# Hybrid trunk on one core: the modulation beside the MLPs becomes row products on VectorE, and the MLP down products come two up products later

## The chip, the cores and the metric

The kernel runs on one core of one Trainium2 chip, as one launch. The metric is the device time of that core in microseconds (us); the median of three runs of the kernel before is 2835.36 us.

## The reference

A trunk of two layers over 256 tokens with 2048 features, in fp32. Each layer is a token mixer (layer 0: sparse attention, called DSA; layer 1: RWKV-7 time mixing), followed by an MLP with 8192 hidden features and a squared ReLU. Every sub-layer reads a norm of x that is shifted and scaled, and what it gives is gated and added to x. The shifts, scales and gates (the modulation, six parts of 2048 numbers a layer) come from one vector c of 2048 numbers:

```python
def block(x, c, mix, ada_w, ada_b, w1, w2):       # cut to what matters here
    sh1, sc1, g1, sh2, sc2, g2 = split(silu(c) @ ada_w + ada_b, 6)   # ada_w: 2048 x 12288
    x = x + g1 * mix(rms_norm(x) * (1 + sc1) + sh1)
    h = rms_norm(x) * (1 + sc2) + sh2
    return x + g2 * (square(relu(h @ w1)) @ w2)                      # w1: 2048 x 8192, w2: 8192 x 2048
```

So ada_w (100.7 MB a layer) is read once for a product with a single row, and w1 and w2 (67.1 MB each a layer) are read once for products with 256 rows.

## The kernel before, in words

**Phases.** The program runs through five phases: `dsa` (with the modulation that layer 0 needs first), `mlp0`, `project` and `scan` (the RWKV mixer), `mlp1`. The features lie across the 128 partitions, 16 tiles of x with 256 tokens each. A scheduler of the framework orders the instructions of every engine ahead of the launch, by priorities that follow the order of the code and by a timeline that it models; at run time each engine takes its instructions strictly in that order. All weight loads are issued by SyncE (SP), in its order too.

**Products.** A weight chunk comes from HBM in 128x512 pieces of 256 KB (tiles `raw` and `more`). Each piece is split into a high part, which ScalarE casts (`whi`, L87), and a low part, which VectorE or GpSimd subtracts (`wlo`, L89; in the MLPs the last two of a chunk's four pieces go to GpSimd, `g=(2, 3)`; some split buffers bear the names `xhi` and `xlo`). A moving tile has a high and a low half too, and each 128-row step of a product is three matmuls (L182 to L184: high x high, high x low, low x high). A product of an MLP sums 16 such steps, 48 matmuls, in one bank of PSUM (`ps_d`, `ps_m`, `ps_a` or `ps_b`).

**The MLP.** Four blocks of 2048 hidden features follow one another; in each, 16 up products (w1) make 16 hidden tiles, and then 16 down products (w2) read all 16 of them. An up product is followed on VectorE and ScalarE by a chain: scale by the tokens' 1/rms (L370), ReLU (L371), square in full (L372) and as a high part (L374), low part (L375). A down product ends in an add into `y` (L384). An MLP is 4 x 32 x 48 = 6144 matmuls.

**The modulation.** `ada_block` makes 512 of the 12288 numbers. Its ada_w block comes in eight loads of 512 KB (`araw`). Of a block there are two ways. The "array" way makes 16 matmuls on TensorE with c as the stationary operand (L215), then a transpose and a few small products. The "vector" way makes 16 multiply-adds over 128x512 into `acc`: the first on ScalarE (L217), 15 on VectorE (L219); then a 32x32 block transpose (L228), a sum (L233), four small products on TensorE (L237) and the add of a bias (L240, in two parts of six also L242). In `dsa` every third block goes the vector way; beside the MLPs all do: 24 blocks beside `mlp0` (the last part of layer 0, and five parts of layer 1) and 4 beside `mlp1`. A queue of generators feeds them in: before each MLP product, `ada_due` adds 0.8 (mlp0) or 0.2 (mlp1) steps, a step being a quarter of a block.

Of the kernel before, what the change touches and what calls it, by code (L numbers as in the profile page):

```python
# [7 lines left out]
F32 = mybir.dt.float32  # L8
F32R = mybir.dt.float32r
# [7 lines left out]
P = 128  # L17
# [21 lines left out]
ADA_INDEX, ADA_TOPK, ADA_HEAD, ADA_OUT = 2, 6, 2, 3    # steps of the modulation beside a step of the DSA mixer  # L39
TAIL = "dcm"        # banks of the DSA mixer's last output products  # L40
# [19 lines left out]
# columns of the constants kept for the whole launch, and of those of the DSA mixer alone  # L60
# [15 lines left out]

class Weights:
    """A chunk of weights as high and low parts, in pieces of up to 512 columns."""
# [18 lines left out]
class Trunk:  # L97
    def __init__(s, ctx, tc, io):
# [17 lines left out]
        s.turn, s.kinds, s.ada_kind = 0, "d", "j"  # L116
# [38 lines left out]
    # weights: a chunk of up to 2048 columns, split exactly in two parts  # L155
    def raw(s, ap, own=True):
        if not own and s.bufs["m"]:
            t = s.tp.tile([P, 1024], F32, name="araw", bufs=s.bufs["m"])
        else:
            s.raws += 1  # L160
            if s.raws % (NRAW + s.bufs["q"]) < NRAW:
                t = s.wp.tile([P, 512], F32, name="raw", bufs=NRAW)[:, :ap.shape[-1]]
            else:
                t = s.tp.tile([P, 512], F32, name="more", bufs=s.bufs["q"])[:, :ap.shape[-1]]
        s.nc.sync.dma_start(t, ap)
        return t
# [32 lines left out]
    # modulation: c_act @ ada_w, four feature tiles at a time  # L199
    def ada_block(s, layer, part, j, where):  # L200
        # where the products are made: in the array, on VectorE, or on ScalarE and GpSimd
        nc = s.nc
        blk = part * 4 + j
        array = where == "array"
        if array:
            # partial sums in the four column tiles of the array
            p = s.bank(s.ada_kind)
        acc = None if array else s.tp.tile([P, 512], F32, name="acc", bufs=1 + (s.bufs["m"] > 2))
        for q in range(4):
            w = [s.raw(s.io["ada_w"][layer, blk, q, :, i * 1024:(i + 1) * 1024], False) for i in range(2)]  # L210
            for k in range(4):
                c = s.cact[:, q * 4 + k:q * 4 + k + 1]
                wk = w[k // 2][:, k % 2 * 512:k % 2 * 512 + 512]
                if array:
                    nc.tensor.matmul(p[k * 32:k * 32 + 32, :], c.to_broadcast([P, 32]), wk, start=q == 0, stop=q == 3)  # L215
                elif q == 0 and k == 0:
                    nc.scalar.activation(acc, wk, AF.Copy, scale=c)  # L217
                elif where == "vector":
                    nc.vector.scalar_tensor_tensor(acc, wk, c, acc, op0=OP.mult, op1=OP.add)  # L219
                else:  # L220
                    t = s.A()
                    nc.scalar.activation(t, wk, AF.Copy, scale=c)
                    nc.gpsimd.tensor_tensor(acc, acc, t, op=OP.add)
            if q < 3:
                yield
        # sums over the partitions: by blocks of 32 on VectorE, then of the four blocks
        t = s.tp.tile([P, 512], F32, name="act", bufs=1)
        nc.vector.transpose(t, p if array else acc)  # L228
        if array:
            t = t.rearrange("p (f c i)->p c f i", c=4, i=32)[:, :, :, 0]  # L230
        else:
            r = s.small(16)
            nc.vector.tensor_reduce(r, t.rearrange("p (b i)->p b i", i=32), axis=AX.X, op=OP.add)  # L233
            t = r.rearrange("p (f c)->p c f", c=4)
        p = s.bank(s.ada_kind)
        for c in range(4):
            nc.tensor.matmul(p[c * 32:c * 32 + 32, :4], s.cv("i32"), t[:, c, :], start=True, stop=True)  # L237
        o = part * 16 + j * 4
        dst = s.mod[layer][:, o:o + 4]
        nc.vector.tensor_tensor(dst, p[:, :4], s.v(f"ada_b{layer}", o, 4), op=OP.add)  # L240
        if part in (1, 4):
            nc.vector.tensor_scalar(dst, dst, 1.0, None, op0=OP.add)  # L242
        yield

    def ada_enqueue(s, layer, parts, where=("vector",)):
        for p in parts:
            for j in range(4):
                s.adaq.append(s.ada_block(layer, p, j, where[j % len(where)]))
# [9 lines left out]
    # 1 / sqrt(sum / n + eps) of sums [128 tokens, w] in PSUM  # L258
# [14 lines left out]
    def spread(s, r, w, kind="m"):  # L273
        # [128 tokens, 2 tiles x w] -> [128 features, 256 tokens], w values over 128 / w features each
# [22 lines left out]
    def rms(s, n, sq):  # L297
        # 1 / rms by token, in every partition; sq: squares
# [9 lines left out]
    def modulated(s, layer, base, i, rb):  # L308
        # x * rstd * (1 + scale) + shift, split
# [27 lines left out]
    def mlp(s, layer):  # L337
        nc = s.nc
        s.kinds = "dcm"
        # the tokens' 1 / rms goes to the products, so that they can start before it is known; the shift  # L340
        # is a further column
# [16 lines left out]
        y = [s.tp.tile([P, S], F32, name=f"y{f}") for f in range(NF)]  # L358
        for b in range(4):
            hid = []  # L360
            for f in range(16):
                w = s.wload(s.io["mlp_w1"][layer, b * 16 + f])
                s.ada_due()
                p = s.dense(w, h, cols)
                if b == f == 0:
                    nc.scalar.copy(rb, s.rms(D, [s.ssq, s.lsq]))
                u, r, q = s.B(), s.B(), s.B()
                c = s.small(1)
                nc.scalar.copy(c, p[:, S:S + 1])
                nc.vector.tensor_tensor(u, p[:, :S], rb, op=OP.mult)  # L370
                nc.scalar.activation(r, u, AF.Relu, bias=c)  # L371
                nc.vector.tensor_tensor(q, r, r, op=OP.mult)  # L372
                t = s.O() if 1 < f < 2 + NO else s.A(F32R)
                nc.scalar.activation(t[:, :S], r, AF.Square)  # L374
                nc.vector.tensor_tensor(t[:, S:], q, t[:, :S].bitcast(F32), op=OP.subtract)  # L375
                hid.append(t)
            for f in range(16):
                w = s.wload(s.io["mlp_w2"][layer, b, f])
                s.ada_due()
                p = s.dense(w, hid, cols)  # L380
                if b == 0:
                    nc.scalar.copy(y[f], p)
                else:
                    nc.vector.tensor_tensor(y[f], p, y[f], op=OP.add)  # L384
                if b == 3:
                    nc.vector.scalar_tensor_tensor(s.x[f], y[f], s.m(layer, 5, f), s.x[f], op0=OP.mult, op1=OP.add)
                    s.tally(f)
# [844 lines left out]
```

## Time and profile before

| what | before |
|---|---|
| median of 3 runs | 2835.36 us (2834.36 to 2837.69) |
| span of the profiled execution | 2835.9 us (no separate time is given for it) |
| TensorE busy | 2666.8 us, 94% |
| VectorE busy | 2009.3 us, 71% |
| ScalarE busy | 1330.1 us, 47% |
| GpSimd busy | 1252.3 us, 44% |
| moved by DMA | 621.70 MB, mean 219 GB/s |

Busy shares are means over five phases with different limits, so the views by stage count for more than this table. A busy time holds also what an instruction waits once it has begun, for a port for example. PE is TensorE, DVE VectorE, ACT ScalarE, POOL GpSimd, SP SyncE.

### The profile page before, as it was taken

To read this page: it belongs to the slowest core of one execution; us is meant where nothing else is said; L and a number is where in the kernel's file an instruction comes from. 1 tells how busy PE (TensorE), PEld (TensorE's weight loads), DVE (VectorE), ACT (ScalarE), POOL (GpSimd) and SP (SyncE) were. 2 spreads that over 40 slices of the span, in tenths; PEclk is the share of its full clock that TensorE was granted. 3 is DMA by queue.
4 is the path that set the end of the run, shared out by engine and by line. 5 is a ranking of instruction groups with operands and counts; after the bars stand their busy time and mean duration, and the time that the engine had idled before them with its cause. 6 is when DMAs were issued, how large, how long until landed. Compare 5 with 4: busy or idle time off the path is not lost. (4 is left out here: it accounts for less than half of the span.)

```text
span 2835.9 us, 65852 instructions
## 1 busy us (share of the span) xinstructions
PE 2666.8 (94%) x25132; PEld 2460.3 (87%) x25132; DVE 2009.3 (71%) x3475; ACT 1330.1 (47%) x2879; POOL 1252.3 (44%) x1121
## 2 busy tenths in 40 slices
PE   7989998899999999998989899999898999999998
PEld 4566688899999999997978788888798999999998
DVE  2276658999999999948887656766798264473653
ACT  3334345445444544446655334444445454454553
POOL 1343237445454454455665412323554444444443
PEclk9998999999999999999999879999999999999999
DMA  9987836999899899854657632333577656555563
GB/s 356 367 305 289 297 106 197 299 312 332 290 302 318 291 312 318 268 174 127 201 174 224 190 91 77 105 113 89 157 262 239 193 182 183 182 182 185 182 182 115
DMA packets 290847, 621.70 MB, mean 219 GB/s; under 512 B 32353, under 2 KB 46049, under 8 KB 290529
## 3 DMA queue, kind: packets, MB, share of 16 engines
q1 hardware_dynamic: 283616, 604.89, 66.0%
q10 hardware_dynamic: 6912, 12.59, 1.2%
q8 instruction: 197, 3.23, 0.5%
q14 instruction: 122, 0.99, 0.1%
HBM read 600.57 MB, written 16.78 MB: 218 GB/s over the span
## 5 line engine op out<-in xcount | busy, mean ns | idle before, releaser
L89 POOL TENSOR_TENSOR wlo<-raw,whi 128x512 fp32r<-128x512 f32 x364 | 515.9, 1423 | 616.5 <-ACT whi L87 439.3
L87 ACT CAST whi<-raw 128x512 fp32r<-128x512 f32 x856 | 516.4, 617 | 453.5 <-PE ps_d L183 158.7
L89 DVE TENSOR_TENSOR wlo<-raw,whi 128x512 fp32r<-128x512 f32 x492 | 412.5, 842 | 236.2 <-ACT whi L87 226.4
L219 DVE SCALAR_TENSOR_TENSOR acc<-araw,cact,acc 128x512 f32<-128x512 f32 x465 | 476.2, 1025 | 8.1 <-ACT acc L217 4.4
L89 POOL TENSOR_TENSOR wlo<-more,whi 128x512 fp32r<-128x512 f32 x181 | 256.0, 1416 | 312.8 <-ACT whi L87 201.2
L87 ACT CAST whi<-more 128x512 fp32r<-128x512 f32 x366 | 223.2, 617 | 218.6 <-PE ps_d L183 75.5
L182 PE MATMUL ps_d<-A,whi 128*128 128x256 f32 x1058 | 312.7, 297 | 12.4 <-ACT B L849 4.6
L183 PE MATMUL ps_d<-A,whi 128*128 128x256 f32 x1058 | 306.1, 290 | 5.7 <-DVE A L196 5.1
L184 PE MATMUL ps_d<-A,wlo 128*128 128x256 f32 x1058 | 303.8, 287 | 0.0
L89 DVE TENSOR_TENSOR wlo<-more,whi 128x512 fp32r<-128x512 f32 (+1 forms) x185 | 152.1, 824 | 141.9 <-ACT whi L87 139.3
L182 PEld LDWEIGHTS ps_d<-A,whi 128*128 128x128 f32 x1058 | 206.0, 195 | 33.3 <-issue 6.5
L183 PEld LDWEIGHTS ps_d<-A,whi 128*128 128x128 f32 x1058 | 206.9, 196 | 10.4 <-DVE A L196 9.0
L184 PEld LDWEIGHTS ps_d<-A,wlo 128*128 128x128 f32 x1058 | 206.5, 195 | 1.4 <-issue 1.4
L183 PE MATMUL ps_d<-h,whi 128*128 128x258 f32 x552 | 157.9, 286 | 2.9 <-DVE h L352 2.8
L184 PE MATMUL ps_d<-h,wlo 128*128 128x258 f32 x552 | 156.8, 284 | 1.9 <-DVE wlo L89 1.9
L182 PE MATMUL ps_d<-h,whi 128*128 128x258 f32 x552 | 157.7, 286 | 0.0
L371 ACT ACTIVATE B<-B,sm 128x256 f32<-128x256 f32 x128 | 65.0, 508 | 197.1 <-DVE B L370 197.0
L182 PE MATMUL ps_m<-h,whi 128*128 128x258 f32 x536 | 153.2, 286 | 0.0
L183 PE MATMUL ps_m<-h,whi 128*128 128x258 f32 x536 | 152.6, 285 | 0.0
L184 PE MATMUL ps_m<-h,wlo 128*128 128x258 f32 x536 | 151.6, 283 | 0.0
L182 PE MATMUL ps_m<-A,whi 128*128 128x256 f32 x510 | 145.6, 286 | 5.4 <-DVE B L372 4.4
L183 PE MATMUL ps_m<-A,whi 128*128 128x256 f32 x510 | 145.0, 284 | 1.5 <-DVE A L375 1.5
(555 smaller groups left out, 8753.1 us busy)
## 6 DMA issues: line engine op xcount, KB each, us to landing
araw<-ada_w_in SPq DMA_DIRECT2D x384, 512.0 KB, 6.3
raw<-mlp_w_in SPq DMA_DIRECT2D x614, 256.0 KB, 4.0
more<-mlp_w_in SPq DMA_DIRECT2D x410, 256.0 KB, 4.2
raw<-b_w_r_in SPq DMA_DIRECT2D x64, 256.0 KB, 3.6
raw<-b_w_k_in SPq DMA_DIRECT2D x64, 256.0 KB, 4.0
raw<-b_w_v_in SPq DMA_DIRECT2D x64, 256.0 KB, 3.7
raw<-b_w_o_in SPq DMA_DIRECT2D x64, 256.0 KB, 3.5
hd<-A ACTq DMA_DIRECT2D x48, 256.0 KB, 4.7
```

The source lines that it names most:

```text
L87: t.nc.scalar.copy(hi[:, :n], r)
L89: e.tensor_tensor(lo[:, :n], r, hi[:, :n].bitcast(F32), op=OP.subtract)
L182: mm(out, wh, m[:, :w], start=i == 0, stop=False)
L183: mm(out, wh, m[:, w:], start=False, stop=False)
L184: mm(out, wl, m[:, :w], start=False, stop=i == n - 1)
L219: nc.vector.scalar_tensor_tensor(acc, wk, c, acc, op0=OP.mult, op1=OP.add)
L371: nc.scalar.activation(r, u, AF.Relu, bias=c)
```

## The change

1. A block of ada_w that went the vector way is now laid out by rows: one of its 512 outputs to a partition, four times over, and its 2048 inputs along the free axis (the host lays the weights out so). `spread_c` broadcasts c to all partitions once in each of three phases and makes silu(c) there, 128x2048 (`cb`). Four row products (`tensor_tensor_reduce`, 128x2048 by `cb`, summed along the row) and one add of the bias then make a block, all on VectorE. The blocks that go the array way stay there, and no block changes its way between the array and VectorE.
2. All ada_w loads are 1 MB (128x2048) in place of 512 KB; the buffers `araw` are 4 of 8 KB a partition in `dsa` in place of 9 of 4 KB, and 2 of 8 KB beside the MLPs in place of 4 of 4 KB.
3. In the MLPs the first two up products of the next block come ahead of a block's 16 down products (`AHEAD_UP = 2`), in the first three of the four blocks.

```diff
+def ada_by_row(layer, part, j):
+    return layer == 1 or part == 5 or (part > 1 and j == 2)
...
+    def spread_c(s):
+        nc = s.nc
+        s.cb = s.tp.tile([P, D], F32, name="cb", bufs=1)
+        nc.sync.dma_start(s.cb, s.io["c"].partition_broadcast(P))
+        sg = s.tp.tile([P, D], F32, name="araw", bufs=s.bufs["m"])
+        nc.scalar.activation(sg, s.cb, AF.Sigmoid)
+        nc.vector.tensor_tensor(s.cb, s.cb, sg, op=OP.mult)
...
+        for k in range(4):
+            w = s.tp.tile([P, D], F32, name="araw", bufs=s.bufs["m"])
+            nc.sync.dma_start(w, s.io["ada_w"][layer, o // 4, k])
+            if by_row:
+                nc.vector.tensor_tensor_reduce(out=w, in0=w, in1=s.cb, scale=1.0, scalar=0.0, op0=OP.mult, op1=OP.add,
+                                               accum_out=acc[:, k:k + 1])
...
+            for f in range(AHEAD_UP if b else 0, 16):
+                up(b, f)
+            for f in range(AHEAD_UP if b < 3 else 0):
+                up(b + 1, f)
+            for f in range(16):
+                down(b, f)
...
-        with t.phase("mlp0", a=14, b=12, w=2, m=4, q=MORE, g=(2, 3)):
+        with t.phase("mlp0", a=14, b=12, w=2, m=2, q=MORE, g=(2, 3)):
+            t.spread_c()
```

The functions `up` and `down` hold what stood in the two loops of `mlp`. Line numbers move by the edit: L89 becomes L94, L182 to L184 become L184 to L186, L370, L372 and L375 become L374, L376 and L379; L224 is the row product, L246 the add of the bias.

How the scheduler orders it, at two places. The first is the order on VectorE some 15 up products into `mlp0`. `acc` and `act` are tiles of the modulation, `sm` its sums, `mod` the finished numbers. Before:

```order
L228 STREAM_TRANSPOSE act<-acc 128x512
L372 TENSOR_TENSOR B<-B 128x256
L219 SCALAR_TENSOR_TENSOR acc<-araw,cact,acc 128x512
L375 TENSOR_TENSOR A<-B,A 128x256
L89 TENSOR_TENSOR wlo<-raw,whi 128x512
L219 SCALAR_TENSOR_TENSOR acc<-araw,cact,acc 128x512
L233 TENSOR_REDUCE sm<-act 128x16
```

And of the change (`ISA` is the row product and the reading of its sum):

```order
L224 ISA araw,sm<-araw,cb 128x2048
L224 ISA sm 128x1
L376 TENSOR_TENSOR B<-B 128x256
L246 TENSOR_TENSOR mod_84<-sm,vec 128x4
L94 TENSOR_TENSOR wlo<-raw,whi 128x512
L379 TENSOR_TENSOR A<-B,A 128x256
```

The transpose and the sum are gone, and so is the hand-over to TensorE that followed them. This is what stood on TensorE before where a block's sums came in, amid the 48 matmuls of an up product:

```order
L182 MATMUL ps_d<-h,whi 128x258
L237 MATMUL ps_j<-sm,cst 32x4 x4
L183 MATMUL ps_d<-h,whi 128x258
L184 MATMUL ps_d<-h,wlo 128x258
L182 MATMUL ps_d<-h,xhi 128x258
```

There are 24 such places in `mlp0` and 4 in `mlp1`, and none in either MLP of the change. The second place is on TensorE, where the up products of block 0 of `mlp0` end (`h` are the tiles that up products read, `A` and `o` the hidden tiles that down products read). Before, the bank `ps_d_6574` takes the last up product:

```order
L182 MATMUL ps_d_6574<-h_5022,whi_6568 128x258
L183 MATMUL ps_d_6574<-h_5022,whi_6568 128x258
L184 MATMUL ps_d_6574<-h_5022,wlo_6569 128x258
L182 MATMUL ps_b_6667<-A_5242,whi_6634 128x256
L183 MATMUL ps_b_6667<-A_5242,whi_6634 128x256
```

And of the change, where `ps_d_6266` takes the last up product of block 0, and `ps_b_6354` and `ps_m_6441` the two of block 1:

```order
L186 MATMUL ps_d_6266<-h_4801,wlo_6261 128x258
L184 MATMUL ps_b_6354<-h_4786,whi_6326 128x258
...
L184 MATMUL ps_m_6441<-h_4801,whi_6432 128x258
L185 MATMUL ps_m_6441<-h_4801,whi_6432 128x258
L186 MATMUL ps_m_6441<-h_4801,wlo_6433 128x258
L184 MATMUL ps_d_6528<-A_5021,whi_6501 128x256
```

Between a block's last up product and its first down product there now stand 96 matmuls.

## Rows read from the trace of the kernel before

**Rows 1.** Windows by stage: span, busy (x count) by engine, clock, DMA share, GB/s.

```profile
0.00:141.80 141.80, 114.89 (x720) 65.66 (x721) 37.45 (x84) 48.33 (x97) 36.94 (x40) 0.99 0.98 361
...
470.50:1281.60 811.10, 769.26 (x6345) 761.98 (x6346) 753.93 (x972) 388.62 (x774) 404.30 (x279) 0.97 0.88 288
...
2047.50:2822.20 774.70, 760.43 (x6258) 757.15 (x6256) 450.50 (x609) 388.05 (x763) 362.45 (x289) 0.98 0.61 192
```

**Rows 2.** Windows, a modulated stretch in which TensorE never stands.

```profile
600.00:728.00 128.00, 128.00 (x1087) 127.40 (x1087) 123.09 (x143) 64.37 (x125) 66.27 (x43) 1.00 0.95 325
```

**Rows 3.** Waits of TensorE in mlp0: us, times, longest.

```profile
PE ps_j L237 <- DVE sm L233: 30.3, 10, 5.0
...
PE ps_b L182 <- ACT A L374: 1.8, 1, 1.8
PE ps_d L182 <- ACT A L374: 1.4, 1, 1.4
PE ps_m L183 <- DVE A L375: 1.4, 1, 1.4
```

**Rows 4.** Timeline of TensorE at one such wait: start, us.

```profile
540.51 0.28 PE L182 MATMUL ps_d<-h,whi 128*128 128x258 f32 x1
545.76 0.29 PE L237 MATMUL ps_j<-sm,cst 128*32 128x4 f32 x8 [4.96 <-DVE sm L233]
545.98 0.58 PE L183 MATMUL ps_d<-h,whi 128*128 128x258 f32 x1
```

**Rows 5.** Timeline of VectorE at the same place.

```profile
539.59 0.70 DVE L228 STREAM_TRANSPOSE act<-acc 128x512 f32<-128x512 f32 x1
540.22 1.48 DVE L372 TENSOR_TENSOR B<-B 128x256 f32<-128x256 f32 x1
...
542.28 1.48 DVE L375 TENSOR_TENSOR A<-B,A 128x256 fp32r<-128x256 f32 x1
...
544.94 0.67 DVE L233 TENSOR_REDUCE sm<-act 128x16 f32<-128x512 f32 x1
```

**Rows 6.** Windows of 12 us behind waits, three of mlp0 and one of mlp1.

```profile
545.76:557.76 12.00, 12.00 (x88) 11.98 (x89) 12.00 (x19) 6.44 (x14) 4.25 (x3) 0.79 0.92 289
579.50:591.50 12.00, 12.00 (x106) 11.98 (x107) 11.96 (x18) 6.10 (x14) 5.61 (x4) 1.00 0.89 294
...
1172.49:1184.49 12.00, 12.00 (x83) 11.98 (x84) 10.74 (x18) 6.50 (x14) 3.87 (x3) 0.73 0.86 267
...
2176.30:2188.30 12.00, 12.00 (x81) 11.51 (x82) 11.69 (x15) 5.75 (x11) 4.62 (x4) 0.75 0.88 267
```

**Rows 7.** Groups of VectorE in mlp0: busy, mean ns, idle before.

```profile
L219 DVE SCALAR_TENSOR_TENSOR acc<-araw,cact,acc 128x512 f32<-128x512 f32 x359 | 369.2, 1028 | 4.6 <-ACT acc L217 1.8
...
L228 DVE STREAM_TRANSPOSE act<-acc 128x512 f32<-128x512 f32 x24 | 16.9, 703 | 0.3
L233 DVE TENSOR_REDUCE sm<-act 128x16 f32<-128x512 f32 x24 | 16.2, 676 | 0.2
```

**Rows 8.** GpSimd's splits in mlp0: min/median/max ns.

```profile
L89 POOL TENSOR_TENSOR wlo<-raw,whi x151: 1274/1511/2108, 480.7 to 1268.4; 128x512 fp32r<-128x512 f32 x151
```

**Rows 9.** Groups of VectorE in attention: a multiply with a sum.

```profile
L633 DVE CUSTOM_DVE_ANT_0 lg<-ps_m,A 128x256 f32<-128x256 f32 x16 | 6.7, 419 | 0.0
...
L633 DVE CUSTOM_DVE_ANT_0 lg<-ps_m,A 128x128 f32<-128x128 f32 x16 | 4.5, 284 | 6.9 <-PE ps_m L628 6.8
...
L633 DVE DVE_READ_ACCUMULATOR2_ANT sm<- 128x1 f32 x32 | 2.6, 82 | 0.0
```

**Rows 10.** Waits of SP's queue within mlp0.

```profile
SPq L165 <- DVE acc L219: 119.7, 120, 3.2
```

**Rows 11.** Waits of TensorE in mlp1.

```profile
PE ps_m L182 <- DVE B L372: 4.4, 1, 4.4
```

**Rows 12.** Groups of VectorE where mlp1 starts.

```profile
L219 DVE SCALAR_TENSOR_TENSOR acc<-araw,cact,acc 128x512 f32<-128x512 f32 x14 | 14.9, 1073 | 0.0
```

**Rows 13.** ScalarE's casts in attention.

```profile
L87 ACT CAST whi<-raw 128x512 fp32r<-128x512 f32 x72 | 42.6, 619 | 37.3 <-PE ps_d L183 18.9 <-issue 8.6 <-PE ps_a L183 2.7
```

More of the change, by code (lines that the diff above doesn't have):

```diff
@@ L39 @@
 ADA_INDEX, ADA_TOPK, ADA_HEAD, ADA_OUT = 2, 6, 2, 3
+AHEAD_UP = 2
 TAIL = "dcm"
@@ L115, in __init__ @@
         s.flip = s.raws = s.pieces = 0
-        s.turn, s.kinds, s.ada_kind = 0, "d", "j"
+        s.turn, s.kinds = 0, "d"
         s.due = s.rate = 0.0
@@ L153, in m, with raw @@
         return s.mod[layer][:, part * 16 + i:part * 16 + i + 1]
-    def raw(s, ap, own=True):
-        if not own and s.bufs["m"]:
-            t = s.tp.tile([P, 1024], F32, name="araw", bufs=s.bufs["m"])
-        else:
[L160 to L164, printed above, removed]
+    def raw(s, ap):
+        s.raws += 1
+        if s.raws % (NRAW + s.bufs["q"]) < NRAW:
+            t = s.wp.tile([P, 512], F32, name="raw", bufs=NRAW)[:, :ap.shape[-1]]
+        else:
+            t = s.tp.tile([P, 512], F32, name="more", bufs=s.bufs["q"])[:, :ap.shape[-1]]
         s.nc.sync.dma_start(t, ap)
@@ L197, in split @@
         return t
-    def ada_block(s, layer, part, j, where):
+    def spread_c(s):
         nc = s.nc
[L203 to L224, printed above, removed]
@@ new lines, in spread_c, with ada_block @@
+        s.cb = s.tp.tile([P, D], F32, name="cb", bufs=1)
[3 more added lines that the diff above has]
+        nc.vector.tensor_tensor(s.cb, s.cb, sg, op=OP.mult)
+    def ada_block(s, layer, part, j):
+        nc = s.nc
+        o = part * 16 + j * 4
+        by_row = ada_by_row(layer, part, j)
+        if by_row:
+            acc = s.small(4)
+        else:
+            p = s.bank("j")
+        for k in range(4):
+            w = s.tp.tile([P, D], F32, name="araw", bufs=s.bufs["m"])
+            nc.sync.dma_start(w, s.io["ada_w"][layer, o // 4, k])
+            if by_row:
+                nc.vector.tensor_tensor_reduce(out=w, in0=w, in1=s.cb, scale=1.0, scalar=0.0, op0=OP.mult, op1=OP.add,
+                                               accum_out=acc[:, k:k + 1])
+            else:
+                for q in range(4):
+                    c = s.cact[:, k * 4 + q:k * 4 + q + 1]
+                    nc.tensor.matmul(p[q * 32:q * 32 + 32, :], c.to_broadcast([P, 32]), w[:, q * 512:(q + 1) * 512],
+                                     start=k == 0, stop=k == 3)
+            if k < 3:
@@ L225, in ada_block @@
                 yield
-        t = s.tp.tile([P, 512], F32, name="act", bufs=1)
-        nc.vector.transpose(t, p if array else acc)
-        if array:
+        if not by_row:
+            t = s.tp.tile([P, 512], F32, name="act", bufs=1)
+            nc.vector.transpose(t, p)
             t = t.rearrange("p (f c i)->p c f i", c=4, i=32)[:, :, :, 0]
-        else:
-            r = s.small(16)
-            nc.vector.tensor_reduce(r, t.rearrange("p (b i)->p b i", i=32), axis=AX.X, op=OP.add)
-            t = r.rearrange("p (f c)->p c f", c=4)
@@ L235, in ada_block @@
[L235 to L242, printed above, removed]
+            p = s.bank("j")
+            for c in range(4):
+                nc.tensor.matmul(p[c * 32:c * 32 + 32, :4], s.cv("i32"), t[:, c, :], start=True, stop=True)
@@ L243, in ada_block, with ada_enqueue @@
+            acc = p[:, :4]
+        dst, b = s.mod[layer][:, o:o + 4], s.v(f"ada_b{layer}", o, 4)
+        if part in (1, 4):
+            nc.vector.scalar_tensor_tensor(dst, acc, 1.0, b, op0=OP.add, op1=OP.add)
+        else:
+            nc.vector.tensor_tensor(dst, acc, b, op=OP.add)
         yield
-    def ada_enqueue(s, layer, parts, where=("vector",)):
+    def ada_enqueue(s, layer, parts):
         for p in parts:
             for j in range(4):
-                s.adaq.append(s.ada_block(layer, p, j, where[j % len(where)]))
+                s.adaq.append(s.ada_block(layer, p, j))
@@ L358, in mlp, with up @@
         y = [s.tp.tile([P, S], F32, name=f"y{f}") for f in range(NF)]
+        hid = {}
+        def up(b, f):
+            w = s.wload(s.io["mlp_w1"][layer, b * 16 + f])
+            s.ada_due()
+            p = s.dense(w, h, cols)
+            if b == f == 0:
+                nc.scalar.copy(rb, s.rms(D, [s.ssq, s.lsq]))
+            u, r, q = s.B(), s.B(), s.B()
+            c = s.small(1)
+            nc.scalar.copy(c, p[:, S:S + 1])
+            nc.vector.tensor_tensor(u, p[:, :S], rb, op=OP.mult)
+            nc.scalar.activation(r, u, AF.Relu, bias=c)
+            nc.vector.tensor_tensor(q, r, r, op=OP.mult)
+            t = s.O() if 1 < f < 2 + NO else s.A(F32R)
+            nc.scalar.activation(t[:, :S], r, AF.Square)
+            nc.vector.tensor_tensor(t[:, S:], q, t[:, :S].bitcast(F32), op=OP.subtract)
+            hid[b, f] = t
@@ L359, in mlp, with down @@
+        def down(b, f):
+            w = s.wload(s.io["mlp_w2"][layer, b, f])
+            s.ada_due()
+            p = s.dense(w, [hid[b, k] for k in range(16)], cols)
+            if b == 0:
+                nc.scalar.copy(y[f], p)
+            else:
+                nc.vector.tensor_tensor(y[f], p, y[f], op=OP.add)
+            if b == 3:
+                nc.vector.scalar_tensor_tensor(s.x[f], y[f], s.m(layer, 5, f), s.x[f], op0=OP.mult, op1=OP.add)
+                s.tally(f)
         for b in range(4):
-            hid = []
+            for f in range(AHEAD_UP if b else 0, 16):
+                up(b, f)
+            for f in range(AHEAD_UP if b < 3 else 0):
+                up(b + 1, f)
@@ L361, in mlp @@
             for f in range(16):
[L362 to L387, printed above, removed]
+                down(b, f)
@@ L478, in dsa @@
             for part in (1, 0):
-                s.adaq.append(s.ada_block(0, part, j, "array"))
+                s.adaq.append(s.ada_block(0, part, j))
             s.ada(4)
@@ L490, in dsa @@
             raw.append(t)
-        s.ada_enqueue(0, [2, 3, 4], ("array", "array", "vector"))
+        s.ada_enqueue(0, [2, 3, 4])
         def lowrank(raw, n, gname):
@@ L1087, in build @@
         t.start()
-        with t.phase("dsa", a=27, b=17, m=9, q=MORE, g=(1, 2)):
+        with t.phase("dsa", a=27, b=17, m=4, q=MORE, g=(1, 2)):
+            t.spread_c()
             t.dsa()
@@ L1105, in build @@
         t.rate = 0.2
-        with t.phase("mlp1", a=14, b=12, w=2, m=4, q=MORE, g=(2, 3)):
+        with t.phase("mlp1", a=14, b=12, w=2, m=2, q=MORE, g=(2, 3)):
+            t.spread_c()
             t.mlp(1)
@@ L1180, in layout @@
     a["kidx_ln"] = ct(np.stack([g["a_kidx_ln_g"][0], g["a_kidx_ln_b"][0]], 1))
-    a["ada_w"] = ct(g["ada_w"].reshape(2, 4, 4, P, 24, 512).transpose(0, 4, 1, 3, 2, 5)).reshape(2, 24, 4, P, 2048)
+    aw = g["ada_w"]
+    rows = aw.transpose(0, 2, 1).reshape(2, 24, 4, P, D)
+    cols = aw.reshape(2, 4, 4, P, 24, 512).transpose(0, 4, 1, 3, 2, 5).reshape(2, 24, 4, P, D)
+    a["ada_w"] = np.stack([np.stack([(rows if ada_by_row(l, b // 4, b % 4) else cols)[l, b] for b in range(24)])
+                           for l in range(2)])
+    a["c"] = ct(g["c"].reshape(-1))
     a["mlp_w1"] = np.stack([tiles(w, 16, P) for w in g["mlp_w1"]])
```

2 lines of the change are left out of this document (1 added, 1 removed).

## The prediction, made before the changed kernel was run

> **What bounds the kernel now.** I read the windows by stage first [rows 1]. Two stages hold changed work for hundreds of microseconds: mlp0, 811.1 us with TensorE busy for 769.3, and mlp1, 774.7 us with TensorE busy for 760.4. Both make the same 6144 matmuls, so what mlp0 takes more, 36 us, is what the modulation costs beside it. The reader should see in the same row that VectorE is busy for 753.9 of mlp0's 811.1 us, nearly as long as TensorE, and that DMA runs at a share of 0.88; in mlp1, with a sixth of the modulation, VectorE has 450.5 and DMA 0.61.
>
> Then TensorE's waits within mlp0 [rows 3]. One line stands out: the four small products L237 wait ten times for the sum L233, 30.3 us in all, up to 5.0 us. Three waits of 1.4 to 1.8 us come where a block's up products end and its down products begin (for L374 and L375); the rest is small. The timelines of one such place say why it lasts. TensorE stands from 540.8 to 545.8 amid the 48 matmuls of an up product [rows 4], as L237 is placed there and the order can't be left. VectorE transposes at 539.59 but reaches L233 only at 544.94, since five other instructions stand in between, two of them on 128x256 for 1.48 us each [rows 5]. So TensorE waits for VectorE's queue, not for the modulation's arithmetic.
>
> Last, the windows of 12 us behind these waits [rows 6]. The one at 579.5 keeps the clock (1.00) and holds 106 matmuls; the one at 545.76 has a granted clock of 0.79 and 88, the one at 1172.49 has 0.73 and 83. I looked at the ten behind the ten waits: the counts lie between those two ends, and together lack about 118 matmuls, at 0.12 us each some 14 us. A wait here costs its own length and half as much again at the lower clock.
>
> **What the change removes.** In mlp0: (a) the L237 waits, 30.3 us; nothing in the MLPs of the change hands a modulation sum to TensorE, so the whole line goes. (b) The small products themselves: 24 places of 0.22 us (545.76 to 545.98 [rows 4]), 5.3 us. (c) The low clock behind (a), 14 us. (d) The waits at three block boundaries, 1.8 + 1.4 + 1.4 = 4.6 us: they lie in the first three blocks, where 96 matmuls (11.5 us) now stand between the last up product and the first reader of its tile. In mlp1: (e) the boundary wait of 4.4 us [rows 11], in block 0, and some 3 us of its low clock (81 matmuls against 106 [rows 6]). (f) Where mlp1 starts, VectorE makes 14 multiply-adds for 14.9 us in the first 35 us [rows 12] between the tiles h that TensorE waits for; the change has one 128x2048 multiply there and puts the row products later. I take 4 us, between 0 (the multiply costs as much) and 6.7 (all waits for h in that stage). Sum removed: 30.3 + 5.3 + 14 + 4.6 + 7.4 + 4 = 65.6 us.
>
> **What it adds.** (g) A row product of 128x2048. Nearest rows: a multiply with a sum takes 419 ns over 256 columns and 284 over 128, and 82 for reading the sum [rows 9]; the slope is 1.055 ns a column, so an estimate of 0.284 + 1920 x 0.00105 = 2.31 us, and 0.08. Its inputs there are one from PSUM and one from SBUF, here both from SBUF; four multiply-adds at their mean of 1.03 us in mlp0, waits included [rows 7], give 4.1 us as an upper bound. I take 2.9 us, the estimate with 0.5 us of waiting, since 3.75 multiply-adds become one instruction and so fewer are caught by GpSimd. VectorE in mlp0 then has 753.9 - 369.2 (L219) - 16.9 (L228) - 16.2 (L233) = 351.6, plus 96 x 2.9 = 278: 630 us of a stage of some 760, in place of 754 of 811. At 4.1 us a piece it has 745, and only from (811 - 351.6) / 96 = 4.8 us would VectorE alone need as long as the stage takes now. So the row products lie beside TensorE's matmuls; if that cover went, each 0.1 us of a row product would cost 9.6 us. (h) c is loaded once more in attention's start, where DMA is full (0.98, 361 GB/s): 1 MB, 2.9 us on the path. (i) Sigmoid and multiply of 128x2048 in mlp0's start: at four casts of 0.619 us [rows 13] and an estimate of 2.3 us, they stand in VectorE's queue between the updates of x that TensorE's last attention products and the first tiles h need. I take 2.5 us, between 0 (VectorE has room there) and 5. In mlp1 the same is within (f). (j) New waits of TensorE where VectorE's queue holds two row products in a row: 9 us, between 0 and 45 (as many and as costly as (a) with (c)). I take the low end's side, for the split tiles of an MLP hold ten pieces, two and a half products of 5.8 us, and PSUM has six banks for products, so a delay of 3 to 6 us is mostly covered, unlike L237, which had no cover at all. Sum added: 2.9 + 2.5 + 9 = 14.4 us. Costs nothing: the reshaped loads of attention, the same bytes in half as many instructions, and as many products of the array way.
>
> **Sum.** 2835.9 (span of the profiled execution, 0.5 us above the median, so no correction) - 65.6 + 14.4 = 2784.7; I forecast 2784 us.
>
> **A rule that speaks against it.** In the rows, a VectorE multiply-add has a mean of 1028 ns in mlp0 [rows 7] and a GpSimd split one of 1511 at the median against 1274 at best [rows 8]; so the two engines hold each other up. The Trainium skill, page "SBUF — State Buffer", section "Who interferes with whom", says that a VectorE instruction with two SBUF inputs and a GpSimd instruction that reads SBUF exclude each other, and whichever starts first keeps the shared ports for its whole length. By that rule a row product of 2.3 us would hold a split for up to 2.3 us where a multiply-add held it for 0.7; the spread of the splits (1274 to 2108) agrees with the rule for holds of 0.7 us, and no run here shows longer ones. By the rule the sum moves toward the first rival below; by the rows alone the elements that pass (24 blocks of 8192 columns in place of 7680) hold the ports about as long in total as now.
>
> **Rivals.** *The waits only move.* GpSimd's splits come late behind row products, and TensorE waits for `wlo` where it waited for L237. For it: VectorE was busy nearly throughout, and the order has row products in pairs. Against it: GpSimd is busy for 404 of 811 us [rows 1], no split is among the long waits of TensorE [rows 3]. If half of (a) and (c) comes back, 22 us beyond (j)'s middle: about 2807 us.
>
> *The loads starve TensorE (slower).* SP issues all loads in order, and with two buffers of 1 MB an ada_w load waits in its queue until the row product before last is done, with the weights behind it; already now SP waits 120 times for L219, 119.7 us [rows 10], each a hold of 1 us, and would wait longer for one instruction of 2.9 us. TensorE without gaps needs 325 GB/s at a DMA share of 0.95 [rows 2]. The modulated stretch moves 226 MB (120 products with 1.05 MB of weights each and 96 loads of 1.05 MB), 697 us at 325 GB/s. At 300 it takes 755 us, which gives 2784 + 58 = 2842 us; it decides below 305 GB/s, and the stage's own mean is 288 now. Against it: attention's start shows 361 GB/s [rows 1], and the loads have 1 MB each.
>
> *The row product is slow (slower).* At two cycles a column, 4.6 us and waits of 0.6, VectorE has 351.6 + 96 x 5.3 = 860 us in mlp0, and the kernel takes about 2880 us. Against it: the slope over columns in [rows 9].
>
> *Nothing changes*: other waits of mlp0 grow until VectorE's length sets the stage again, at 4.8 us a row product: 2836 us.
>
> **How the numbers follow.** A change of 0.2% (5.7 us) is about what a measurement of this kernel can tell from none. Forecast, 2766 to 2800: 0.56. Better still (j near 0 and the array part quicker): 0.04. Waits only move, 2800 to 2829: 0.22. Within 0.2%: 0.06. Loads starve: 0.07. Slow row product: 0.05. So faster 0.82, same 0.06, slower 0.12. The range takes the forecast's cases from 2764 and most of the moved waits, up to 2824.
>
> **What would show it.** Right: mlp0 near 765 us, no wait of TensorE for a modulation sum, granted clock 0.99 or 1.00 within mlp0, row products of 2.3 to 3 us, VectorE near 630 us there, no waits of TensorE at the first three boundaries of either MLP, mlp1 near 763. Wrong: waits of TensorE for `wlo` or for weights' DMA of tens of microseconds in mlp0; SP waiting for the row product while ScalarE waits for `raw`; row products above 4 us; attention longer by more than 5 us.

## The result, and the profile after

The changed kernel takes 2787.81 us (median of 4 runs, 2783.42 to 2791.43) where the kernel before takes 2836.53: a ratio of 0.983, with a 95% interval of 0.980 to 0.985. Measured again (experiment e8) the same kernel gave 0.981 (0.979 to 0.984). The forecast was 2784 us. The sum was right; the experiments show that a large step behind it was not.

The windows by stage after the change (attention, mlp0, the RWKV mixer, mlp1; columns as in [rows 1]; each MLP runs from the first product that reads an `h` tile to the sums of squares behind its last product):

```profile
0.00:460.90 460.90, 402.21 (x2820) 298.19 (x2820) 234.38 (x549) 182.50 (x411) 155.43 (x167) 0.94 0.78 286
460.90:1242.30 781.40, 753.77 (x6156) 749.57 (x6157) 716.57 (x751) 371.00 (x762) 495.01 (x281) 0.98 0.87 301
1242.30:2020.70 778.40, 722.02 (x9683) 647.44 (x9681) 549.41 (x1294) 372.16 (x921) 315.21 (x391) 0.93 0.46 138
2020.70:2775.00 754.30, 750.99 (x6216) 750.23 (x6217) 449.54 (x573) 383.29 (x759) 378.90 (x283) 1.00 0.62 196
```

By the same marks the stages before were 470.5, 811.5, 765.5 and 774.2 us. So mlp0 is 30.1 us shorter (forecast: 46), mlp1 19.9 (forecast: 11), attention 9.5 (forecast: 5 longer), and the mixer 12.9 longer, whose code no edit touches (e8 and the text under the table come back to it). VectorE has 717 us in mlp0 where 630 were forecast, and GpSimd went from 404 [rows 1] to 495 us, with one split more (254).

The waits of TensorE in mlp0 after the change (us, times, longest), which answer to [rows 3]:

```profile
PE ps_b L184 <- ACT A L378: 5.3, 1, 5.3
PE ps_d L186 <- DVE wlo L94: 5.3, 3, 2.2
PE ps_m L186 <- DVE wlo L94: 3.7, 1, 3.7
PE ps_d L185 <- DVE h L356: 3.7, 5, 1.6
PE ps_a L185 <- DVE h L356: 2.9, 1, 2.9
PE ps_a L186 <- DVE wlo L94: 2.7, 1, 2.7
```

No wait for a modulation sum is left. The 5.3 us are the boundary of the last block, which has no up products ahead; some 12 us are waits for low parts of weights, of which [rows 3] has none of that size.

VectorE's splits in mlp0 before, and then VectorE's and GpSimd's groups after the change, which answer to [rows 7] and [rows 8] (in the last two fences: min/median/max ns):

```profile
L89 DVE TENSOR_TENSOR wlo<-raw,whi 128x512 fp32r<-128x512 f32 x157 | 148.8, 950 | 24.7 <-ACT whi L87 24.7
```

```profile
L224 DVE CUSTOM_DVE_ANT_0 araw<-araw,cb 128x2048 f32<-128x2048 f32 x96 | 270.7, 2830 | 4.3 <-DMA araw<-ada_w_in 4.3
L94 DVE TENSOR_TENSOR wlo<-raw,whi 128x512 fp32r<-128x512 f32 x157 | 161.3, 1034 | 20.6 <-ACT whi L92 19.0 <-DMA more<-mlp_w_in 1.6
```

```profile
L224 DVE CUSTOM_DVE_ANT_0 araw<-araw,cb x96: 2276/2876/3392, 484.4 to 1184.6; 128x2048 f32<-128x2048 f32 x96
```

```profile
L94 POOL TENSOR_TENSOR wlo<-raw,whi x152: 1287/1740/3438, 460.6 to 1228.8; 128x512 fp32r<-128x512 f32 x152
```

A row product takes 2.28 us at best and 2.83 in the mean: the forecast took 2.31 and 2.9. But the splits of GpSimd now take up to 3.44 us where 2.11 was the longest [rows 8], and VectorE's own splits went from a mean of 950 to 1034 ns. One place shows it (start, duration), TensorE, VectorE and GpSimd:

```profile
582.80 0.28 PE L185 MATMUL ps_d<-o,whi 128*128 128x256 f32 x1
585.27 0.39 PE L186 MATMUL ps_d<-o,wlo 128*128 128x256 f32 x1 [2.19 <-DVE wlo L94]
```

```profile
577.92 3.38 DVE L224 CUSTOM_DVE_ANT_0 araw<-araw,cb 128x2048 f32<-128x2048 f32 x1
...
581.24 3.37 DVE L224 CUSTOM_DVE_ANT_0 araw<-araw,cb 128x2048 f32<-128x2048 f32 x1
...
584.53 0.68 DVE L94 TENSOR_TENSOR wlo<-raw,whi 128x512 fp32r<-128x512 f32 x1
```

```profile
577.78 4.67 POOL L94 TENSOR_TENSOR wlo<-raw,whi 128x512 fp32r<-128x512 f32 x2 [0.33 <-ACT whi L92]
```

Two row products start while GpSimd splits; each takes 1.1 us more than its shortest, and GpSimd's two splits take 4.67 us where two at their best take 2.6. The low part that TensorE needs stands behind them. This is the rule of the Trainium skill (page "SBUF — State Buffer", section "Who interferes with whom") that the prediction weighed: a VectorE instruction with two SBUF inputs contends with a GpSimd instruction that reads SBUF, and the ports that they share are an exclusive lock. The trace agrees, and shows that a whole instruction can be waited for: the longest split is now 2.15 us over its shortest, about one row product (2.28), and was 0.83 over it before, about one multiply-add (0.75 in e12).

### The profile page after: what moved, and what is told of

Its sections match the earlier page's. It is cut to its first block, busy times and chain, and to the rows that moved or that the text cites. A ratio compares the mean times of both kernels' runs of the same rounds, so it can differ in the third digit from the quotient of the medians.

```text
span 2788.7 us, 64443 instructions
## 1 busy us (share of the span) xinstructions
PE 2630.8 (94%) x24884; PEld 2446.9 (88%) x24884; DVE 1957.3 (70%) x3183; ACT 1309.4 (47%) x2852; POOL 1345.3 (48%) x1121
## 5 line engine op out<-in xcount | busy, mean ns | idle before, releaser
L94 POOL TENSOR_TENSOR wlo<-raw,whi 128x512 fp32r<-128x512 f32 x364 | 587.1, 1622 | 544.5 <-ACT whi L92 417.2
L94 DVE TENSOR_TENSOR wlo<-raw,whi 128x512 fp32r<-128x512 f32 x492 | 436.5, 892 | 222.6 <-ACT whi L92 211.0
L94 POOL TENSOR_TENSOR wlo<-more,whi 128x512 fp32r<-128x512 f32 x181 | 263.7, 1460 | 322.7 <-ACT whi L92 165.6
L224 DVE CUSTOM_DVE_ANT_0 araw<-araw,cb 128x2048 f32<-128x2048 f32 x124 | 342.6, 2776 | 4.6 <-DMA araw<-ada_w_in 4.6
L184 PE MATMUL ps_d<-A,whi 128*128 128x256 f32 x1058 | 309.4, 293 | 10.6 <-ACT B L863 6.2
L186 PE MATMUL ps_d<-A,wlo 128*128 128x256 f32 x1058 | 303.1, 287 | 0.5 <-DVE wlo L94 0.5
L94 DVE TENSOR_TENSOR wlo<-more,whi 128x512 fp32r<-128x512 f32 (+1 forms) x185 | 174.3, 943 | 138.8 <-ACT whi L92 135.6
L184 PEld LDWEIGHTS ps_d<-A,whi 128*128 128x128 f32 x1058 | 205.4, 195 | 26.2 <-ACT B L863 7.2
L186 PEld LDWEIGHTS ps_d<-A,wlo 128*128 128x128 f32 x1058 | 205.5, 194 | 1.5 <-DVE wlo L94 0.7
L375 ACT ACTIVATE B<-B,sm 128x256 f32<-128x256 f32 x128 | 65.3, 510 | 247.5 <-DVE B L374 247.4
L186 PE MATMUL ps_d<-h,wlo 128*128 128x258 f32 x552 | 155.8, 282 | 2.5 <-DVE wlo L94 2.4
L184 PE MATMUL ps_d<-h,whi 128*128 128x258 f32 x552 | 156.7, 284 | 0.0
L184 PE MATMUL ps_m<-h,whi 128*128 128x258 f32 x540 | 153.4, 284 | 0.0
L186 PE MATMUL ps_m<-h,wlo 128*128 128x258 f32 x540 | 152.1, 282 | 0.0
L376 DVE TENSOR_TENSOR B<-B 128x256 f32<-128x256 f32 x128 | 111.5, 871 | 52.9 <-ACT B L375 52.9
L184 PE MATMUL ps_m<-A,whi 128*128 128x256 f32 x506 | 145.1, 287 | 1.1 <-ACT whi L92 1.1
```

Source lines behind the costliest of these rows:

```text
L94: e.tensor_tensor(lo[:, :n], r, hi[:, :n].bitcast(F32), op=OP.subtract)
L184: mm(out, wh, m[:, :w], start=i == 0, stop=False)
L186: mm(out, wl, m[:, :w], start=False, stop=i == n - 1)
L224: nc.vector.tensor_tensor_reduce(out=w, in0=w, in1=s.cb, scale=1.0, scalar=0.0, op0=OP.mult, op1=OP.add, accum_out=acc[:, k:k + 1])
```

## The experiments

All use the whole kernel and the reference's inputs; e6 alone leaves out a part of the result. Ratios are to the kernel before, measured beside them.

| kernel | attention | mlp0 | mixer | mlp1 | VectorE busy in mlp0 | ratio (95%) |
|---|---|---|---|---|---|---|
| before | 470.5 | 811.5 | 765.5 | 774.2 | 753.9 | 1 |
| the change | 460.9 | 781.4 | 778.4 | 754.3 | 716.6 | 0.983 (0.980 to 0.985) |
| e1 change, nothing ahead | 459.9 | 798.8 | 769.8 | 760.4 | 674.6 | 0.990 (0.988 to 0.992) |
| e2 before, two ahead | 463.9 | 814.2 | 767.8 | 773.3 | 758.4 | 1.002 (1.0005 to 1.004) |
| e3 before, hand-over later | 468.6 | 821.6 | 767.7 | 773.8 | 750.8 | 1.005 (1.003 to 1.007) |
| e4 before, 1 MB loads | 462.4 | 813.0 | 781.4 | 771.4 | 754.7 | 1.002 (1.001 to 1.004) |
| e5 = e2 + e3 | 471.0 | 814.4 | 770.5 | 772.6 | 757.6 | 1.001 (1.0002 to 1.003) |
| e6 change, no row products | 454.7 | 749.9 | 772.4 | 755.0 | 402.2 | 0.970 (0.968 to 0.973) |
| e7 change, last boundary split | 460.7 | 780.7 | 780.2 | 755.2 | 718.9 | 0.983 (0.980 to 0.985) |
| e8 change again | 466.8 | 783.4 | 765.5 | 755.0 | 715.5 | 0.981 (0.979 to 0.984) |
| e9 change, splits on VectorE | 466.4 | 746.9 | 762.8 | 753.0 | 644.6 | 0.971 (0.968 to 0.973) |
| e10 change, square on ScalarE | 460.9 | 775.1 | 783.3 | 756.1 | 690.8 | 0.980 (0.978 to 0.982) |
| e11 before, square on ScalarE | 472.4 | 793.3 | 771.2 | 774.8 | 720.4 | 0.995 (0.994 to 0.997) |
| e12 before, splits on VectorE | 470.4 | 751.8 | 789.1 | 760.2 | 692.4 | 0.982 (0.980 to 0.985) |

Stage lengths are of one profiled execution each. Across these kernels the mixer, whose code is the same in all of them, lies between 763 and 789 us, so a few us in a stage are read only where they repeat. The same code is not the same order: the scheduler orders the whole program, and an edit ahead of the mixer moves the mixer's instructions too. By the traces, before, e2, e5 and e11 have nearly one order there (766 to 771 us), the change, e1, e6, e7, e8 and e10 another (765 to 783 us), and e3, e4, e9 and e12 one each (763 to 789 us).

**e1: the row products alone.**

```diff
-AHEAD_UP = 2
+AHEAD_UP = 0
```

> The change without its second part: AHEAD_UP = 0, so down products follow at once behind a block's up products. If the boundary waits are what the early up products take away, they come back: in mlp0 and mlp1 one of 1.5 to 5 us at most boundaries, some with a lower clock behind, together 8 to 18 us, so about 2796 to 2806 us against 2788. If the early up products bring nothing, 2788 us.

Measured 2807.81 us, 20 us more than the change where 8 to 18 were expected. mlp0 is 17.4 us longer than in the change, mlp1 6.1; the waits for L378 at the boundaries are back (TensorE in mlp0):

```profile
PE ps_b L184 <- ACT A L378: 13.3, 3, 5.7
PE ps_m L184 <- ACT A L378: 6.3, 2, 4.3
```

Before, the same boundaries cost 4.6 us [rows 3]. The early up products are thus worth more with the row products than the old boundary waits.

**e2: the up products ahead alone.** `up`, `down` and their order as in the change, everything else as before.

> The kernel before with the second part alone: AHEAD_UP = 2, the modulation as before. By the terms of the prediction the three boundary waits of mlp0 (4.6 us) and that of mlp1 with its clock (7.4 us) go: 2836 - 12 = 2824 us, the waits for L233 stay at some 30 us. The rival: the up products ahead only move the waits for L233 elsewhere, no change.

Measured 2842.87 us, no gain. The boundary waits are gone, and the waits for the sum (L234 here, L233 before) have grown from 30.3 [rows 3] to 37.5 us in mlp0; in mlp1 one of 5.5 us stands where the boundary wait of 4.4 [rows 11] was:

```profile
PE ps_j L238 <- DVE sm L234: 37.5, 10, 5.3
```

```profile
PE ps_m L238 <- DVE sm L234: 5.5, 1, 5.5
```

**e3: the hand-over alone.** The four small products and the bias are issued three products after the sum:

```diff
-        p = s.bank(s.ada_kind)
-        for c in range(4):
...
+        def hand(t=t):
+            p = s.bank(s.ada_kind)
+            for c in range(4):
...
+        if array or not s.rate:
+            hand()
+        else:
+            s.late.append([2, hand])
```

> The kernel before, in which beside the MLPs alone the four small products L237 and the add of the bias are issued three products later; multiply-adds, transposes, loads are all as before. If TensorE lost its time to the place of L237 in its queue, the line of waits for L233 (30 us) and the clock behind it (14 us) go without any row product: mlp0 some 44 us shorter, 2790 to 2800 us. The rival: VectorE's and GpSimd's load sets mlp0's length, then other waits (for low parts of weights, for hidden tiles) take their place and the time stays above 2820 us.

Measured 2847.86 us, 0.5% slower: the rival's case. This is the experiment in which the prediction's main step fell. VectorE's modulation stays within one product of its place before. No wait for a sum is left in mlp0, and TensorE waits as long at the block boundaries (L388 is the high part of the square, L374 before):

```profile
PE ps_b L183 <- ACT A L388: 17.7, 4, 5.1
PE ps_m L183 <- ACT A L388: 8.2, 2, 4.2
PE ps_d L183 <- ACT A L388: 7.1, 2, 4.4
```

**e4: the larger loads alone.** `araw` of 128x2048, loaded at once, 4 and 2 buffers, all else as before.

> The kernel before, in which only the loads of ada_w change: 1 MB in place of 512 KB, with 4 buffers of 8 KB a partition in attention and 2 beside the MLPs. If the larger loads are why attention got shorter (379 GB/s in place of 361 in its first 142 us), attention is 8 to 20 us shorter and mlp0 and mlp1 are as before: 2816 to 2828 us. The rivals: attention got shorter since the blocks by rows took multiply-adds from VectorE, then no change, 2836 us; or two large buffers hold up SP's queue in mlp0, then mlp0 is longer by 10 us and more.

Measured 2844.65 us: no gain in the time. mlp0 and mlp1 stay, so two large buffers hold nothing up there. Attention was 462 us in its profile, at 375 GB/s in the first 142 us where before had 361 [rows 1]. Over all profiles of the table attention has a mean of 469.5 us with the old loads (6 profiles, 463.9 to 472.4) and 461.6 with the large ones (8, 454.7 to 466.8): probably some 8 us. The timed runs of e4 do not confirm them; in its profile the mixer, in an order of its own, took 781.4 us where before had 765.5, which is more than attention gave.

**e5: both moves, no row products.**

> The kernel before with both moves and no row product: the small products L237 three products later beside the MLPs, and two up products ahead of a block's down products. Alone, neither gained anything: the wait left the one meeting place of TensorE and VectorE and came back at the other. If the two meeting places are the whole cause and VectorE has room enough between them, mlp0 falls by some 30 us as in the change: 2795 to 2810 us. If VectorE's load in mlp0 (750 us of work and held instructions) sets its length, TensorE waits at a third place (low parts of weights, banks of PSUM) and the time stays above 2825 us.

Measured 2842.26 us: no gain. TensorE now meets VectorE at the splits themselves (and at the last boundary, 8.6 us), and waits there some thirty times, mostly for under a us (three of the lines, and the window of mlp0):

```profile
PE ps_d L186 <- DVE wlo L90: 8.5, 11, 2.0
PE ps_m L186 <- DVE wlo L90: 4.4, 5, 1.4
...
PE ps_b L186 <- DVE wlo L90: 3.3, 6, 0.9
```

```profile
471.00:1285.40 814.40, 771.93 (x6348) 752.46 (x6349) 757.63 (x972) 379.14 (x774) 415.07 (x279) 0.99 0.87 287
```

The clock is 0.99 in place of 0.97, and mlp0 is no shorter, so the higher clock gave nothing back here. What stays is VectorE: from the modulation's first to its last instruction in mlp0 it is busy for 720 of 733 us, as before for 715 of 731 (98% in both). A window of before within that stretch:

```profile
496.00:1200.00 704.00, 666.06 (x5507) 660.66 (x5506) 688.02 (x873) 337.36 (x674) 341.93 (x224) 0.97 0.92 305
```

So VectorE sets the length of mlp0 before, in e2 and in e5.

**e6: the change without row products.** A copy of one column stands in for each of the 112 beside the MLPs (96 in mlp0), so this kernel leaves out their part of the modulation.

```diff
-            if by_row:
+            if by_row and s.rate:
+                nc.vector.tensor_copy(acc[:, k:k + 1], w[:, 0:1])
+            elif by_row:
```

> The change, but beside the MLPs a row product is replaced by a copy of one column, so loads, buffers and orders are as in the change and VectorE's 100 long instructions are left out (the modulation that they make is too). If VectorE's load still sets mlp0 in the change, mlp0 comes near mlp1's 754 us, 20 to 28 us shorter: 2760 to 2770 us. If the loads through SP's queue are what is left, mlp0 stays near 780 us: 2785 us.

Measured 2751.14 us; mlp0 750 us at a clock of 1.00, as short as mlp1 (755), and more of a gain than the 20 to 28 us expected. With the loads and SP's queue as in the change, nothing of them shows, and GpSimd's splits alone cost nothing either. The row products beside them still cost the change 31 us in mlp0 and none in mlp1.

**e7: the last boundary.** In block 3 the first two down products are each made in two parts, 13 steps of both and then the last three of both.

```diff
+            for ks in (range(13), range(13, 16)):
+                for f in range(2):
+                    for k in ks:
...
+            if b == 3:
+                down2(b)
```

> The change, and in the last block, which has no up products to put ahead, the first two down products are made in two parts: 13 steps of each, then the last three steps of each, in two banks. The wait there (5.3 + 1.6 us in mlp0, and the lower clock of 0.91 behind it) is then covered by 4.7 us: 4 to 9 us shorter than the change, 2779 to 2784 us, if the hidden tiles are late by those 7 us alone; no gain if VectorE's chain is late at the next product too.

Measured 2788.8 us, no gain: a wait of 5.3 us became one of 4.7 us for the last low part (L379), one of 2.7 for a split, and a few smaller ones.

**e8: the change again.**

> The change once more, unaltered, on the same chip as the others of this call, to see how far its time and the length of its stages vary: attention 461 us, mlp0 781, the RWKV mixer 778, mlp1 754 in its first profile. The mixer's instructions are not edited: if its 13 us more than before are chance (its clock differs from run to run), it is nearer to 766 here; if the other addresses or orders that the change brings are the cause, it is 778 again.

Measured 2784.93 us. mlp0 (783.4) and mlp1 (755.0) repeat within 2 us; the mixer is 765.4 us at a clock of 0.95 where it was 778.4 at 0.93, with the same order of instructions. So the 13 us lie within what the mixer varies by between two executions of one kernel; whether the change's order there adds a few, the profiles do not settle:

```profile
1250.20:2015.60 765.40, 707.46 (x9682) 635.87 (x9680) 549.33 (x1294) 370.48 (x921) 314.52 (x391) 0.95 0.47 141
```

**e9: no GpSimd beside the MLPs.**

```diff
-        with t.phase("mlp0", a=14, b=12, w=2, m=2, q=MORE, g=(2, 3)):
+        with t.phase("mlp0", a=14, b=12, w=2, m=2, q=MORE, g=()):
```

and the same for mlp1.

> The change, with GpSimd's splits beside the MLPs made on VectorE too: in mlp0 254 more instructions there, at 0.68 us each 173 us. If the two engines only hold each other up in turn (VectorE's instructions in the change's mlp0 take some 236 us more than their shortest: 52 in the row products at 2830 against 2289 ns, 108 in its own splits, the rest in short ones), that held time goes with GpSimd's splits: 717 - 236 + 173 = 654 us on VectorE, mlp0 750 to 775 us, 2755 to 2785 us in all. If VectorE's instructions are long for another reason, the 173 us come on top: VectorE above 850 us, mlp0 above 860, slower than 2860 us.

Measured 2749.41 us, the fastest kernel here, 3.0% below before, and a little below the range that was expected if the holding goes. The row products stand within two products of where the change has them. VectorE has 254 more splits in mlp0 and is busy 72 us less; all 96 row products take 2277 to 2292 ns (the window of mlp0, one line of its groups, and the row products' min/median/max):

```profile
466.40:1213.30 746.90, 743.51 (x6157) 742.32 (x6158) 644.60 (x1004) 386.29 (x758) 27.66 (x28) 1.00 0.90 314
```

```profile
L94 DVE TENSOR_TENSOR wlo<-raw,whi 128x512 fp32r<-128x512 f32 x309 | 207.7, 690 | 48.1 <-ACT whi L92 45.8 <-DMA raw<-b_w_r_in 0.7
```

```profile
L224 DVE CUSTOM_DVE_ANT_0 araw<-araw,cb x96: 2277/2284/2292, 484.8 to 1154.0; 128x2048 f32<-128x2048 f32 x96
```

One engine alone does in 645 us what two did in 717 and 495. mlp0 is at e6's floor although it makes the whole modulation. With GpSimd's splits and no row products (e6) mlp0 takes 750 us, with row products and no splits on GpSimd (e9) 747, and only with both 781.

**e10 and e11: less work on VectorE.** The full square of the chain (L376, L372 before; 52 and 41 us of VectorE's busy time in mlp0) goes to ScalarE, in the change and in the kernel before.

```diff
-            nc.vector.tensor_tensor(q, r, r, op=OP.mult)
+            nc.scalar.activation(q, r, AF.Square)
```

> The change, with the full square of the MLP's chain (128x256, 64 in each MLP; 52 us of VectorE in mlp0) made on ScalarE, which is busy for 371 of mlp0's 781 us, at some 0.5 us each. If VectorE's load still sets mlp0 in the change (750 us without the row products, 781 with them), mlp0 loses 8 to 25 us: 2765 to 2780 us. If what is left there is the place of a few waits and not the load, no change, 2785 to 2790 us.

> The kernel before, with the same one move: the full square on ScalarE, 41 us less on VectorE in mlp0, modulation and order of products as before. If VectorE's load sets mlp0 before, this alone shortens it by about what it takes off, some 20 to 40 us: 2798 to 2818 us, and the waits for L233 shrink with it. If the places of L237 and of the block boundaries are what counts, the waits stay as they are: 2832 to 2842 us.

Measured 2777.29 us (e10) and 2822.22 us (e11). In e10 mlp0 is 6 to 8 us shorter and the time 8 to 10; the interval overlaps that of the change, so it is likely and no more. In e11 the time is 11 us and mlp0 18 us shorter, both a little under the lower end of what was expected; VectorE has 33.5 us less, and the waits for L233, where both engines keep the order of before within a product, shrink from 30.3 [rows 3] to 19.5 us:

```profile
PE ps_j L237 <- DVE sm L233: 19.5, 8, 4.1
```

**e12: the kernel before without GpSimd beside the MLPs.** The same edit as in e9.

> The kernel before, with GpSimd's splits beside the MLPs made on VectorE, and nothing else changed. The change with this move had 645 us on VectorE in mlp0, every row product at 2284 ns, and mlp0 at 747 us. Here the 359 multiply-adds should come down from a mean of 1028 to some 735 ns, and VectorE has about 754 - 225 (held) + 172 (253 splits at 0.68 us) = 700 us in mlp0. If the holding alone was the cost, mlp0 falls to 760 to 780 us though all multiply-adds, transposes and places of L237 stay: 2785 to 2810 us. If the multiply-adds' own 264 us and the hand-over are a cost beside it, VectorE has little room and mlp0 stays above 795 us: above 2820 us.

Measured 2783.83 us, as fast as the change and a little below the expected range. mlp0 falls to 751.8 us although all multiply-adds, transposes and hand-overs are still made; TensorE's whole list of waits in mlp0 is one line (the window of mlp0, the multiply-adds, the waits):

```profile
470.40:1222.20 751.80, 751.56 (x6348) 747.57 (x6349) 692.37 (x1224) 395.78 (x773) 22.06 (x24) 1.00 0.92 310
```

```profile
L219 DVE SCALAR_TENSOR_TENSOR acc<-araw,cact,acc 128x512 f32<-128x512 f32 x359 | 266.0, 747 | 8.8 <-ACT acc L217 4.5 <-DMA araw<-ada_w_in 4.1
```

```profile
PE ps_d L182 <- ACT h L351: 0.8, 1, 0.8
```

The edit moves more than it names. The scheduler counts on VectorE making the splits and puts L237 up to five products later on TensorE, some three in the mean (the second behind 644 matmuls of mlp0 where before has it behind 466), and VectorE's modulation some three products later. So in mlp0 e12 does not tell what the old places of L237 would cost without GpSimd; a later place alone gained nothing (e3, e5). In mlp1 the four L237 stand behind the same numbers of matmuls as before, and mlp1 is 14 us shorter too.

Its mixer, in an order of its own, took 789 us in the profile, at a clock of 0.93, the longest of all. With the mixer of before the other stages would give some 2762 us, and no timed run of e12 is under 2780: so here the mixer is not long by chance alone, and why stays open.

## Why the prediction was right, and where it was not

**The time** (2784 forecast, 2788 measured) and the range held. That is partly luck: mlp0 gained 16 us less than forecast, mlp1 9 more, attention 9 to 15 more, and the mixer, for which nothing was forecast, took 13 us back in one profile of the change and none in the other.

**The step that failed** is the reading of the waits: "So TensorE waits for VectorE's queue, not for the modulation's arithmetic", with the terms (a) 30.3 and (c) 14 us. VectorE's queue was late indeed; what failed is to take the waits at L237 for time that goes when L237 goes. e3 took those waits away without a row product and gained nothing; e2 took the boundary waits (d) and (e) away, and gained nothing; e5 took both and most of the low clock away, and gained nothing. The waits are where TensorE's order shows that VectorE is behind, not why. That terms (a) to (d) sum to 54 us of the 62 that mlp0 stood over e6's floor says little: what TensorE takes over a floor shows up as waits and low clock somewhere, whatever the cause. (One of the ten windows behind (c) holds 77 matmuls, below the two ends named, since another wait of 1.6 us falls in it; the 118 allow for that.)

**What stands in its place.** In mlp0 before, VectorE and GpSimd hold each other up: the multiply-adds take 1028 ns in the mean, and 747 when GpSimd is out of the way (e12); for 359 that is 101 us of VectorE's time, and its other instructions with two SBUF inputs are held too (the full squares 645 ns, 417 in e12). With that gone, all work of the modulation may stay and mlp0 falls by 60 us (e12). As the order moves too in e12, the cleaner trials are e9, with the row products in their places (34.5 us), e12's mlp1, and e11, in which less work on VectorE alone shortens mlp0 in the old order. The multiply-adds' own time, 266 us, hides behind TensorE in e12.

**How the change gains, then.** It makes one instruction of 3.75, and leaves out the transposes and sums. Alone (e1) that takes VectorE in mlp0 from 754 to 675 us and mlp0 from 811.5 to 798.8; with the up products ahead 781.4. The order ahead is worth 17 us there, not the 4.6 us of term (d), and nothing without the row products (e2). The likely reason: VectorE is busy for 86% of the modulated stretch in e1 and 98% in e2, so in e1 it is late for a while and catches up, which 96 matmuls ahead can cover, and in e2 it is behind throughout.

**VectorE's load (g).** The row product was sized well (2.9 forecast, 2.83 and 0.08 for the read measured). The sum of 630 us failed since it left the other instructions as they were, and so did the thought that the ports would be held about as long in total: VectorE's other instructions take 438 us in place of 351.6 and GpSimd's splits 466 in place of 385, and VectorE has 717 us. So the first rival, the waits that only move, came true in part: some 12 us of waits for `wlo`, and 31 us over the floor (e6) where (j) put 9. The slack that the forecast saw, some 130 us, was not there.

**mlp1.** Terms (e) and (f), 11.4 us, were undersized: 19.9 and 19.2 us in two profiles. The two-ahead order alone gives 1 us (e2), the row products 14 (e1), the move of the splits without either 14 (e12). Taking away either the multiply-adds or GpSimd's splits gives those 14 us, so here too it is the two side by side. 753 to 756 us, where the change and e6 to e10 all stand, looks like the floor.

**Attention.** The 2.9 us for c (h) and 2.5 (i) are not to be seen. ScalarE does wait 13.6 us for c and TensorE 19.5 us for the squares behind it, but the sums are done at 33.3 us where they were at 32.7: before, TensorE waited there for loads. The 8 us in the other direction go with the 1 MB loads, which e4 has without any row product (462 us); why larger loads help stays open.

**The slower rivals** did not come: the loads keep up even at 314 GB/s in e9's mlp0, 310 in e12's, and no row product came near 4.6 us.

## What to carry to other kernels

A wait names the place where an engine that is behind gets noticed. Before a wait is priced as a gain, move that place alone, or take load off the suspected engine alone; in these runs the first gave nothing and the second paid. When two engines share work, compare each instruction's mean with its shortest: where the gap is wide on both, the second engine may take away more than it gives, and the trial was one line for each MLP here. Where a scheduler orders the whole program, look at what else an edit moved: e12 moved the hand-over too, and several edits moved the mixer.

## What the runs showed of the hardware

Moving 254 instructions from GpSimd to VectorE made VectorE's busy time fall (717 to 645 us in mlp0, e9); the row products, VectorE instructions with two SBUF inputs, lay between 2276 and 3392 ns beside GpSimd's splits and between 2277 and 2292 ns without them. The RWKV mixer, whose code no kernel here edits, took 763 us at a granted clock of 0.95 (e9) and 789 us at 0.93 (e12) in two orders of its instructions, and in two executions of the change, in one order, 778 at 0.93 and 765 at 0.95.
